# Latent squares summed by TensorE, key tiles taken when the token products leave PSUM, and the second memory tile of the cross values two steps behind the first

## The chip, the cores and the metric

The kernel runs on one core of a Trainium2 chip. The metric is device time in microseconds (us) of one execution, and less is better. The core has a matmul engine (TensorE, PE in the rows; PEld is its weight load), a vector engine (VectorE, DVE), an engine for activations and copies (ScalarE, ACT), a general engine (GpSimd, POOL) and one that issues the transfers (SyncE, SP). Each runs its own program in order and waits on the others through semaphores.

## The reference

```python
for l in range(DEPTH):                                  # DEPTH = 2, SEQ = 512, D_MODEL = 1024
    h = h + hybrid_mixer(rmsnorm(h, attn_norm[l]), ...)
    h = h + memory_cross_attention(rmsnorm(h, cross_norm[l]), rmsnorm(mem, mem_norm[l]), ...)
    h = h + squared_relu_mlp(rmsnorm(h, mlp_norm[l]), mlp_w1[l], mlp_w2[l])
return rmsnorm(h, final_norm)
...
# hybrid_mixer: three groups of heads read one projection n @ w_in
c_q, c_kv, k_r, dq, dk, dv, mq, mk, mv = jnp.split(proj, cuts, axis=-1)
qh = to_heads(rmsnorm(c_q, q_norm) @ w_uq, 96)          # MLA, 6 heads; c_q is 256 wide
kvh = to_heads(rmsnorm(c_kv, kv_norm) @ w_ukv, 128)     # c_kv is 128 wide
k_rope = apply_rope(k_r[:, None], pos)                  # one rotary key for all 6 heads
...
lam = jnp.exp(jnp.sum(lq1 * lk1)) - jnp.exp(jnp.sum(lq2 * lk2)) + lam_init
p = probs(q1, k1) - lam * probs(q2, k2)                 # differential heads, 6
...
# memory_cross_attention: 4 heads over a memory of 256 rows
kv = mem_n @ wkv
```

The third group has 4 block-sparse heads (MoBA). All self-attention is causal, and all arithmetic is float32.

## The kernel before

A float32 product is made of three passes over rounded pieces: every operand is split into an upper half (a cast) and a lower half (the rest, made by a subtraction), and `mm3` issues upper by upper, upper by lower and lower by upper into one PSUM bank. So each weight tile that arrives by DMA is cast by ScalarE (L157), gets its lower half from GpSimd or VectorE (L162), and only then feeds TensorE; there are 5 such pairs of tiles (`w`), 4 buffers for what arrives (`raw`), and 21 pairs for activations (`B`, split at L140/L142, or L144/L145 with a scale). PSUM has three rotating groups of banks: `mm` (3), `s` (3) and `t` (2).

Each layer begins with the mixer. Its projections are generators ("fill") in the order `kv cq tok m0 d0 m1 d1 o0 m2 d2 o1 mem cross`, and the attention units of a group of heads run between their steps once they can. Work that hangs on a product and would stall the engines is put off by a count of "ticks" with `after(ticks, call)`; TensorE's steps count the ticks. Last, a scheduler moves instructions within each engine's program, so the order written is not always the order run.

The stages that the change touches, in the order in which they run:

- `kv` and `cq` make the latents: one tile of 128 rows for kv, two for q. ScalarE copies each product out of PSUM (L760) and squares it (L762). For q, VectorE adds the two squares (L764). Then `column_sums` multiplies the squares by a matrix of ones on TensorE (8 passes with 2 columns), which gives the sum for each token; a reciprocal root follows, and `rows` scales the latent and splits it (kind "lat", lower half on GpSimd).
- `tok` makes, token by token, the differential values and the rotary key: 4 token tiles by 8 steps of the inner dimension by 3 passes of 288 columns, in four PSUM banks (two of `mm`, two of `s`). Its `evict` splits the values out of PSUM (L144, L145), `rotate` turns the key by its position (L825 to L828), and `turn` transposes it (L280 on TensorE), copies it out (L837), splits it (kind "kr") and takes four pairs of `B` for the key tiles.
- `m0`, `m1`, `m2` make q and k of the MLA heads, two heads at a time (L880 scales q by a table and splits it, kind "mq"). Then come the scores of a unit of 128 queries (L638 on VectorE adds the bias and finds the largest, L640 on ScalarE is the exponential with its sum), a reciprocal (L699), a scaling (L700; on GpSimd for the second of the four units), transposes of the probabilities by TensorE (L280), and the product with the values.
- `d0` to `d2` are the differential heads: two score maps per unit, the factor between them from two reciprocals (L1000, L1001), a third one for the end (L1002), and L703, which joins the maps. The factor needs `neg_lam`, which `setup_lambda` makes once from a small transfer: four products of 32 columns (L481), four reductions (L482), an Exp (L483) and four ops with one column.
- `cross` (`cross_memory_steps`, which runs as fill of the mixer) makes keys and values of the memory. For the values, each of two column halves `c` takes two `mm` banks, one for each memory tile `t`, and at each of 8 steps `k` both tiles use one weight tile.

## Time and profile before

| what | value |
|---|---|
| median of 3 runs | 1529.4 us (1529.02 to 1532.49) |
| the profiled execution | 1527.16 us |
| its span, first to last instruction | 1525.3 us |
| TensorE busy | 1481.2 us, 97% of the span |
| VectorE, ScalarE, GpSimd busy | 70%, 56%, 24% |
| mean granted TensorE clock | 0.994 of full speed |

The busy share says which engine has the least room, not what a single stall costs; for that each stage's own rows are needed, and of them the time in which TensorE stood idle and what it waited for. The granted clock is the share of full speed that TensorE was given in a stretch. The profiled execution is 2.2 us under the median.

### The profile page before, as it was taken

The numbers are of one execution on the slowest core, as the hardware profiler recorded it, in microseconds if no ns is written. First come the engines' busy times: TensorE is split into PE (matmuls) and PEld (weight loads), VectorE is DVE, ScalarE is ACT, GpSimd is POOL, SyncE is SP. The second block draws the span as 40 slices with busy tenths as digits, with TensorE's granted clock in tenths as the row PEclk, the third lists the DMA queues.
The fourth block names the chain that finished last, engine by engine and source line by source line (L and its number), as shares of the span: only waits on it lengthen the run. The fifth ranks groups of instructions, "written<-read, shape, count | busy, mean of one in ns | idle before, by whom it ended". The sixth has DMA issues, their size and how long they took to land.

```text
span 1525.3 us, 24601 instructions
## 1 busy us (share of the span) xinstructions
PE 1481.2 (97%) x8648; PEld 1295.4 (85%) x8648; DVE 1060.3 (70%) x2422; ACT 856.9 (56%) x1887; POOL 365.3 (24%) x302
## 2 busy tenths in 40 slices
PE   7899999999999999999999999999999999999997
PEld 6778897888899899998897888878888989899887
DVE  7688888536699666675537898873378976677753
ACT  5666777535566544454446677764366654445441
POOL 2645375442000000000145446644400000000001
PEclk9999999999999999999999999999999999999998
DMA  4434543231223323322224535423212332333331
GB/s 153 127 106 138 153 132 111 77 96 49 87 74 125 111 88 105 100 96 98 96 77 112 150 113 154 118 86 95 98 34 76 106 123 90 104 96 106 111 97 55
DMA packets 90139, 157.24 MB, mean 103 GB/s; under 512 B 12065, under 2 KB 17057, under 8 KB 90017
## 3 DMA queue, kind: packets, MB, share of 16 engines
q1 hardware_dynamic: 89728, 155.63, 33.2%
q8 instruction: 68, 1.11, 0.3%
q14 instruction: 55, 0.44, 0.1%
q10 hardware_dynamic: 288, 0.05, 0.0%
HBM read 136.24 MB, written 2.10 MB: 91 GB/s over the span
## 4 chain that ended last, share of the span: by engine, by line
PE 71%; DVE 10%; issue 9%; ACT 4%; DMA 3%; POOL 2%; SPq 0%; POOLq 0%; DVEq 0%; ACTq 0%
PE mm L277 58%; PE s L277 10%; PE t L280 2%; DMA raw<-w 2%; DVE tmp L638 1%; ACT tmp L640 1%; DVE tmp L703 1%; POOL w L162 1%; DVE pt L663 1%; ACT B L140 1%; DMA raw<-w_in 1%; DVE small L1001 1%; POOL B L142 1%; PE t L277 1%; DVE tmp L261 1%
## 5 line engine op out<-in xcount | busy, mean ns | idle before, releaser
L277 PE MATMUL mm<-B,w 128*128 128x512 f32 (+1 forms) x2490 | 574.4, 386 | 1.3 <-POOL B L142 1.3
L277 PEld LDWEIGHTS mm<-B,w 128*128 128x128 f32 x2490 | 453.0, 189 | 95.1 <-POOL B L142 2.6
L277 PE MATMUL mm<-A,w 128*128 128x512 f32 (+1 forms) x1920 | 386.7, 351 | 6.2 <-ACT A L144 5.8
L157 ACT CAST w<-raw 128x512 fp32r<-128x512 f32 (+1 forms) x372 | 225.1, 607 | 269.6 <-PE mm L277 208.0
L277 PEld LDWEIGHTS mm<-A,w 128*128 128x128 f32 x1920 | 311.8, 190 | 50.7 <-ACT A L144 5.8
L162 POOL TENSOR_TENSOR w<-raw,w 128x512 fp32r<-128x512 f32 (+2 forms) x180 | 228.0, 1273 | 220.1 <-ACT w L157 177.9
L410 POOL TENSOR_TENSOR tmp<-tmp,tmp 128x512 f32<-128x512 f32 (+1 forms) x25 | 30.8, 1234 | 655.7 <-ACT tmp L407 653.6
L162 DVE TENSOR_TENSOR w<-raw,w 128x512 fp32r<-128x512 f32 x192 | 134.4, 700 | 35.5 <-ACT w L157 35.2
L640 ACT ACTIVATE tmp<-tmp,small 128x384 f32<-128x384 f32 (+3 forms) x176 | 99.0, 562 | 66.0 <-DVE small L638 63.2
L1080 DVE TENSOR_TENSOR h<-mm,h 128x512 f32<-128x512 f32 x92 | 63.3, 688 | 70.9 <-PE mm L277 70.6
L140 ACT CAST B<-tmp 128x512 fp32r<-128x512 f32 (+2 forms) x156 | 91.9, 591 | 24.1 <-DVE tmp L680 4.8
L277 PE MATMUL mm<-pt,B 128*128 128x256 f32 x768 | 102.9, 283 | 2.4 <-ACT tmp L1319 2.4
L277 PEld LDWEIGHTS mm<-pt,B 128*128 128x128 f32 x768 | 95.8, 189 | 3.4 <-ACT tmp L1319 3.4
L261 DVE TENSOR_TENSOR tmp<-raw,raw 128x512 f32<-128x512 f32 x64 | 44.0, 688 | 65.9 <-DMA raw<-w 65.9
L264 ACT CAST B<-tmp 128x512 fp32r<-128x512 f32 x96 | 59.5, 620 | 50.8 <-DVE tmp L261 50.8
L142 DVE TENSOR_TENSOR B<-tmp,B 128x512 fp32r<-128x512 f32 (+1 forms) x110 | 75.5, 686 | 12.3 <-ACT B L140 8.3
L280 PE MATMUL t<-ident,tmp 128*128 128x128 f32 (+1 forms) x444 | 74.5, 274 | 9.3 <-DVE tmp L828 3.3
L280 PEld LDWEIGHTS t<-ident,tmp 128*128 128x128 f32 (+1 forms) x444 | 54.2, 140 | 24.8 <-issue 4.2
L142 POOL TENSOR_TENSOR B<-tmp,B 128x512 fp32r<-128x512 f32 (+1 forms) x46 | 61.4, 1340 | 49.7 <-ACT B L140 47.4
L663 DVE TENSOR_TENSOR pt<-t,pt 128x256 fp32r<-128x256 f32 (+1 forms) x192 | 67.1, 370 | 6.3 <-ACT pt L660 5.4
L277 PE MATMUL s<-pt,B 128*128 128x512 f32 (+3 forms) x352 | 71.0, 345 | 0.0
L339 POOL TENSOR_TENSOR small<-small,mhalf 128x4 f32<-128x4 f32 (+2 forms) x19 | 23.4, 1229 | 198.2 <-DVE small L373 174.5
(195 smaller groups left out, 2135.8 us busy)
## 6 DMA issues: line engine op xcount, KB each, us to landing
raw<-w SPq DMA_DIRECT2D x256, 256.0 KB, 2.9
raw<-w_in SPq DMA_DIRECT2D x64, 256.0 KB, 3.0
st<-B SPq DMA_DIRECT2D x144, 64.0 KB, 2.0
raw<-w_ck SPq DMA_DIRECT2D x32, 256.0 KB, 2.9
raw<-w_cv SPq DMA_DIRECT2D x32, 256.0 KB, 2.7
raw<-w_out SPq DMA_DIRECT2D x32, 256.0 KB, 2.7
raw<-w_cq SPq DMA_DIRECT2D x32, 256.0 KB, 2.7
raw<-w_co SPq DMA_DIRECT2D x32, 256.0 KB, 2.6
```

Source lines behind the costliest of these rows:

```text
L140: nc.scalar.copy(hi, x)
L142: eng.tensor_tensor(lo, x, hi.bitcast(F32), ALU.subtract)
L157: self.nc.scalar.copy(w[:, 0, :], raw)
L162: eng.tensor_tensor(w[:, 1, :], raw, w[:, 0, :].bitcast(F32), ALU.subtract)
L261: nc.vector.tensor_tensor(got[name], x, y, op)
L264: nc.scalar.copy(w[:, 0, :], raw)
L277: self.in_order(self.nc.tensor.matmul(out, lhs, rhs, start=start, stop=stop, skip_group_check=open), hold)
L280: self.in_order(self.nc.tensor.transpose(out, x, self.ident))
L410: eng.tensor_tensor(s[:, :n], s[:, :n], self.sq[:, :n], ALU.add)
L640: nc.scalar.activation(t[:, :n], t[:, :n], AF.Exp, bias=st[:, 0:1], scale=-1.0, accum_out=st[:, 1:2])
L663: nc.vector.tensor_tensor(lo, src, hi.bitcast(F32), ALU.subtract)
L1080: nc.vector.tensor_tensor(self.h[m], ps, self.h[m], ALU.add)
```

## The change

`column_sums` takes a list of squares and lets TensorE add them up in PSUM: for q, 16 passes instead of 8, and no add on VectorE. `token_steps` takes three banks of `s` and one of `mm`, and its four pairs of `B` for the keys as soon as `evict` runs; the scores of an MLA head wait (by running ticks) until `turn` has been issued, which is put off by 6 ticks instead of 2. The exponential writes its sum straight into the tile that collects the sums, so one reciprocal over 8 columns serves a pair of differential heads in place of eight over one column, and the scaling of the second unit (L700) goes from GpSimd to VectorE. `setup_lambda` makes its products in one op over 128 columns and one reduction, and is issued at tick 44 in place of 58; the parts of `setup_distances` start at tick 28 in place of 24. In the cross values the second memory tile runs two steps behind the first.

```diff
-    def column_sums(self, sq, ones, ntok, w):
+    def column_sums(self, sqs, ones, ntok, w):
...
         for j in range(ntok):
-            self.mm(o[:, j * w:(j + 1) * w], sq[:, j * P:(j + 1) * P], ones, True, True)
+            for i, sq in enumerate(sqs):
+                self.mm(o[:, j * w:(j + 1) * w], sq[:, j * P:(j + 1) * P], ones, i == 0, i == len(sqs) - 1)
...
-        prod, dots, ex = self.small(64), self.small(4), self.small(4)
-        for l in range(L):
-            for j in range(2):
-                o = (l * 4 + 2 * j) * 32
-                nc.vector.tensor_tensor(prod[:, :32], v[:, o:o + 32], v[:, o + 32:o + 64], ALU.mult)
-                nc.vector.tensor_reduce(dots[:, 2 * l + j:2 * l + j + 1], prod[:, :32], mybir.AxisListType.X, ALU.add)
+        prod, dots, ex = self.small(128), self.small(4), self.small(4)
...
+        nc.vector.tensor_tensor(prod, pairs[:, :, 0, :], pairs[:, :, 1, :], ALU.mult)
+        nc.vector.tensor_reduce(dots, prod, mybir.AxisListType.X, ALU.add)
         nc.scalar.activation(ex, dots, AF.Exp)
...
-        nc.scalar.activation(t[:, :n], t[:, :n], AF.Exp, bias=st[:, 0:1], scale=-1.0, accum_out=st[:, 1:2])
-        return t, st[:, 1:2]
+        nc.scalar.activation(t[:, :n], t[:, :n], AF.Exp, bias=st[:, 0:1], scale=-1.0, accum_out=sums)
+        return t
...
-                (nc.gpsimd if i == 1 else nc.vector).tensor_scalar_mul(t[:, :n], t[:, :n], r)
+                nc.vector.tensor_scalar_mul(t[:, :n], t[:, :n], r)
...
-                if sq is not None:
-                    nc.vector.tensor_tensor(s, s, sq, ALU.add)
-                sq = s
+                sqs.append(s)
...
-            ps = [self.psum("mm"), self.psum("mm"), self.psum("s"), self.psum("s")]
+            ps = [self.psum(t) for t in ("s", "s", "s", "mm")]
...
             def evict():
+                self.keys += [self.pair("B") for _ in range(4)]
...
-                first = self.pair("B")
+                first = self.keys[0]
                 self.split(first[64:128, 0, :], first[64:128, 1, :], u[64:128, :], kind="kr")
-                self.keys.append(first)
-                for j in range(3):
-                    kt = self.pair("B")
+                for kt in self.keys[1:]:
                     nc.sync.dma_start(kt[64:128].bitcast(F32), first[64:128].bitcast(F32))
-                    self.keys.append(kt)
+                self.turned = True
...
                 def terms(e=e):
+                    while not self.turned:
+                        self.tick()
...
-                    nc.vector.reciprocal(r1()[:, 2 * i + e:2 * i + e + 1], s1)
...
-                ot, r = o(), r1()
+                ot, r = o(), self.small(8)
+                nc.vector.reciprocal(r, sums())
...
-            for k in range(KT):
-                w = self.weights(a["w_cv"][l, c * KT + k])
-                for t in range(2):
-                    ts = slice(t * P, (t + 1) * P)
-                    self.mm3(ps[t], (mem[k][0][:, ts], mem[k][1][:, ts]), (w[:, 0, :], w[:, 1, :]),
-                             k == 0, k == KT - 1)
-                    yield 640
+            ws = []
+            for j in range(KT + 2):
+                if j < KT:
+                    ws.append(self.weights(a["w_cv"][l, c * KT + j]))
+                for t, k in ((0, j), (1, j - 2)):
+                    if 0 <= k < KT:
+                        ts, w = slice(t * P, (t + 1) * P), ws[k]
+                        self.mm3(ps[t], (mem[k][0][:, ts], mem[k][1][:, ts]), (w[:, 0, :], w[:, 1, :]),
+                                 k == 0, k == KT - 1)
+                        yield 640
...
-        self.chain_n, self.chain_l, self.chain_d, self.chain_k = 6, 12, 4, 2
+        self.chain_n, self.chain_l, self.chain_d, self.chain_k = 6, 12, 4, 6
...
-            self.after(24 + 2 * n, part)
-        self.after(58, self.setup_lambda)
+            self.after(28 + 2 * n, part)
+        self.after(44, self.setup_lambda)
```

The first place is TensorE's program in layer 0 around the sum of the q latent's squares. `t_89` (now `t_79`) is the sum, `tmp_78` was the sum of both squares; `tmp_51` and `tmp_70` are now the two squares. The products of 288 columns are the token products. Before:

```order
L277 MATMUL mm_79_407<-w_84_413,A_7_129 128x288 x3
L277 MATMUL mm_80_408<-w_84_413,A_7_129 128x288 x3
L277 MATMUL s_81_409<-w_84_413,A_7_129 128x288 x3
L277 MATMUL s_82_410<-w_84_413,A_7_129 128x288 x3
L277 MATMUL mm_79_407<-w_88_438,A_8_132 128x288 x3
L277 MATMUL t_89_447<-ones2_93,tmp_78_404 128x2 x4
L277 MATMUL mm_80_408<-w_88_438,A_8_132 128x288 x3
```

And of the change:

```order
L277 MATMUL s_71_388<-w_54_314,A_5_123 128x288 x3
L277 MATMUL s_72_389<-w_54_314,A_5_123 128x288 x3
L277 MATMUL s_73_390<-w_54_314,A_5_123 128x288 x3
L277 MATMUL mm_74_391<-w_54_314,A_5_123 128x288 x3
L277 MATMUL s_71_388<-w_61_345,A_6_126 128x288 x3
L277 MATMUL s_72_389<-w_61_345,A_6_126 128x288 x3
L277 MATMUL t_79_420<-ones2_93,tmp_51_309 128x2
L277 MATMUL t_79_420<-ones2_93,tmp_70_386 128x2
...
L277 MATMUL s_73_390<-w_61_345,A_6_126 128x288 x3
```

The sums stood behind 13 of the 32 groups of token products and now stand behind 6; the first group that needs an `mm` bank is the fourth, where it was the first.

The second place is GpSimd's program in layer 0, where the lower halves of q and of the rotary key are made. `B_112`, `B_116` and `B_117` are the latents of kv and q, `B_134` (before) and `B_122` (now) the key with its rotary half, `B_140`/`B_143` and `B_142`/`B_145` the two heads of q. Before:

```order
L142 TENSOR_TENSOR B_112_572<-tmp_25_208,B_112_572 128x512
L162 TENSOR_TENSOR w_129_671<-raw_128_669,w_129_671 128x512
L142 TENSOR_TENSOR B_116_604<-tmp_50_307,B_116_604 128x512
L142 TENSOR_TENSOR B_117_608<-tmp_77_402,B_117_608 128x512
L162 TENSOR_TENSOR w_151_752<-raw_150_750,w_151_752 128x512
L162 TENSOR_TENSOR w_159_785<-raw_158_783,w_159_785 128x512
L142 TENSOR_TENSOR B_134_697<-tmp_133_695,B_134_697 64x512
L162 TENSOR_TENSOR w_170_821<-raw_169_819,w_170_821 128x512
L162 TENSOR_TENSOR w_189_900<-raw_188_898,w_189_900 128x256
L142 TENSOR_TENSOR B_140_715<-tmp_139_713,B_140_715 128x512
```

And of the change, from the same place:

```order
L142 TENSOR_TENSOR B_112_575<-tmp_25_208,B_112_575 128x512
L162 TENSOR_TENSOR w_133_678<-raw_132_676,w_133_678 128x512
L142 TENSOR_TENSOR B_116_607<-tmp_50_307,B_116_607 128x512
L142 TENSOR_TENSOR B_117_611<-tmp_69_384,B_117_611 128x512
L162 TENSOR_TENSOR w_156_768<-raw_155_766,w_156_768 128x512
L162 TENSOR_TENSOR w_165_802<-raw_164_800,w_165_802 128x512
L142 TENSOR_TENSOR B_142_718<-tmp_141_716,B_142_718 128x512
L142 TENSOR_TENSOR B_145_730<-tmp_144_728,B_145_730 128x512
L142 TENSOR_TENSOR B_122_636<-tmp_147_738,B_122_636 64x512
```

The rotary key's lower half stood ahead of both halves of q and now stands behind them. On ScalarE, the table load for the exponential and `setup_lambda`'s Exp now stand between the casts of the two heads of q; before they stood behind them.

The third place is TensorE's program in layer 0 where the cross values go from the first column half to the second. `mm_724` and `mm_725` (now `mm_776` and `mm_777`) are the two memory tiles of the first half, `mm_788` and `mm_789` (now `mm_845` and `mm_846`) those of the second, which takes the third bank and then the one of the first tile. Before:

```order
L277 MATMUL mm_724_3070<-w_765_3214,A_593_2486 128x512 x3
L277 MATMUL mm_725_3071<-w_765_3214,A_593_2486 128x512 x3
L277 MATMUL mm_788_3302<-w_775_3250,A_587_2465 128x512 x3
L280 MATMUL t_793_3313<-ident_88,tmp_756_3186 128x128
L277 MATMUL s_794_3317<-st_470_1995,st_444_1896 128x512
L277 MATMUL s_797_3323<-st_470_1995,st_444_1896 128x512
L277 MATMUL mm_788_3302<-w_785_3287,A_587_2465 128x512 x3
L277 MATMUL mm_788_3302<-w_791_3306,A_589_2472 128x512 x3
L277 MATMUL mm_788_3302<-w_802_3339,A_589_2472 128x512 x3
L277 MATMUL mm_789_3303<-w_775_3250,A_587_2465 128x512 x3
```

And of the change:

```order
L277 MATMUL mm_776_3102<-w_820_3240,A_634_2509 128x512 x3
L277 MATMUL mm_777_3103<-w_794_3159,A_632_2502 128x512 x3
...
L277 MATMUL mm_777_3103<-w_806_3192,A_634_2509 128x512 x3
L277 MATMUL mm_777_3103<-w_820_3240,A_634_2509 128x512 x3
L277 MATMUL mm_845_3334<-w_822_3251,A_628_2488 128x512 x3
L280 MATMUL t_850_3345<-ident_88,tmp_813_3224 128x128
L277 MATMUL s_852_3350<-st_499_2009,st_471_1910 128x512
L277 MATMUL s_855_3356<-st_499_2009,st_471_1910 128x512
L277 MATMUL mm_845_3334<-w_833_3287,A_628_2488 128x512 x3
L277 MATMUL mm_845_3334<-w_848_3338,A_630_2495 128x512
L277 MATMUL mm_846_3335<-w_822_3251,A_628_2488 128x512
```

The first tile of the first half now ends nine passes of TensorE (with transposes and scores between them) ahead of the second one, and the last bank is first written after seven passes of the second half instead of twelve.

## Rows read from the trace of the kernel before

**Rows 1.** The page, busy times, shares of the span and instructions.

```profile
PE 1481.2 (97%) x8648; PEld 1295.4 (85%) x8648; DVE 1060.3 (70%) x2422; ACT 856.9 (56%) x1887; POOL 365.3 (24%) x302
```

**Rows 2.** TensorE's waits by cause: total us, times, longest us.

```profile
PE s L277 <- DVE small L638: 4.1, 6, 1.2
...
PE mm L277 <- DVE B L145: 2.2, 2, 1.1
```

**Rows 3.** TensorE from 28 to 56 us: start, length, instructions, idle time and releaser.

```profile
29.43 0.67 PE L277 MATMUL mm<-w,A 128*128 128x288 f32 x3 [0.67 <-ACT tmp L760]
...
37.29 1.02 PE L277 MATMUL t<-ones,tmp 128*128 128x2 f32 x8 [2.86 <-DVE tmp L764]
...
48.62 1.45 PE L277 MATMUL t<-w,B 128*128 128x128 f32 x12
...
51.06 0.97 PE L277 MATMUL mm<-B,w 128*128 128x512 f32 x3 [0.71 <-POOL B L142]
52.32 2.11 PE L277 MATMUL mm<-B,w 128*128 128x512 f32 x8 [0.29 <-POOL B L142]
55.32 0.63 PE L280 MATMUL t<-ident,tmp 128*64 128x128 f32 x4 [0.90 <-DVE tmp L828]
```

**Rows 4.** ScalarE's squares and VectorE's add of the q latent, layer 0.

```profile
31.30 0.58 ACT L760 COPY tmp<-mm 128x512 f32<-128x512 f32 x1
...
32.88 0.63 ACT L762 ACTIVATE tmp<-tmp 128x512 f32<-128x512 f32 x1
...
36.47 0.68 DVE L764 TENSOR_TENSOR tmp<-tmp,tmp 128x512 f32<-128x512 f32 x1
```

**Rows 5.** GpSimd in layer 0, lower halves of the latents.

```profile
41.15 1.27 POOL L162 TENSOR_TENSOR w<-raw,w 128x512 fp32r<-128x512 f32 x1 [0.68 <-ACT w L157]
43.32 0.81 POOL L593 TENSOR_SCALAR_AFFINE_SELECT dneg<-dneg 128x128 f32<-128x128 f32 x1 [0.90 <-DVE small L776]
...
49.74 2.53 POOL L142 TENSOR_TENSOR B<-tmp,B 128x512 fp32r<-128x512 f32 x2
```

**Rows 6.** Three stretches: engines' busy time, granted clock (PEclk), DMA share, GB/s.

```profile
38.00:44.00 6.00, 6.00 (x36) 6.00 (x37) 4.47 (x12) 2.48 (x5) 4.07 (x5) 0.72 0.23 57
76.00:82.00 6.00, 5.60 (x21) 4.73 (x22) 5.03 (x16) 2.58 (x9) 1.01 (x1) 0.72 0.34 80
806.00:812.00 6.00, 5.13 (x18) 4.14 (x19) 3.36 (x6) 2.97 (x5) 3.03 (x3) 0.72 0.30 87
```

**Rows 7.** TensorE in the first MLA heads' units, layer 0.

```profile
68.50 0.44 PE L280 MATMUL t<-ident,tmp 128*128 128x128 f32 x2 [1.18 <-POOL tmp L700]
...
76.40 0.63 PE L280 MATMUL t<-ident,tmp 128*128 128x128 f32 x4 [2.38 <-DVE tmp L700]
```

**Rows 8.** VectorE's wait for the lambda transfer, and ScalarE's table load, layer 0.

```profile
71.27 0.19 DVE L481 TENSOR_TENSOR small<-tmp 128x32 f32<-128x32 f32 x1 [1.39 <-DMA tmp<-lam]
...
61.45 1.28 ACT L640 ACT_TABLE_LOAD   x1
62.75 0.40 ACT L640 ACTIVATE tmp<-tmp,small 128x128 f32<-128x128 f32 x1
```

**Rows 9.** Layer 1: TensorE at the turn of the rotary key; VectorE's rotation.

```profile
806.87 0.63 PE L280 MATMUL t<-ident,tmp 128*64 128x128 f32 x4 [2.43 <-DVE tmp L828]
...
805.31 1.24 DVE L827 TENSOR_TENSOR tmp<-tmp,tmp 128x64 f32<-128x64 f32 x1
```

**Rows 10.** Cross values in layer 0: TensorE's wait, VectorE's lower halves.

```profile
246.09 1.65 PE L277 MATMUL mm<-w,A 128*128 128x512 f32 x6 [1.11 <-DVE B L145]
...
245.30 1.40 DVE L145 SCALAR_TENSOR_TENSOR B<-mm,rcol,B 128x512 fp32r<-128x512 f32 x2
```

**Rows 11.** Lines L1002 and L700: ns shortest/median/longest, first and last start, forms.

```profile
L1002 DVE RECIPROCAL r<-small x48: 135/157/165, 89.5 to 992.3; 128x1 f32<-128x1 f32 x48
...
L700 DVE TENSOR_SCALAR tmp<-tmp,small x60: 276/486/1528, 64.1 to 1015.8; 128x128 f32<-128x128 f32 x20, 128x384 f32<-128x384 f32 x20, 128x512 f32<-128x512 f32 x20
L700 POOL TENSOR_SCALAR tmp<-tmp,small x20: 922/931/1362, 67.5 to 1010.5; 128x256 f32<-128x256 f32 x20
```

More of the change, by code (lines that the diff above doesn't have):

```diff
@@ L627, in stacks, with scores @@
         return tiles, calls
-    def scores(self, i, terms, bias, slope):
+    def scores(self, i, terms, bias, slope, sums):
         nc = self.nc
@@ L694, in start @@
             n = (i + 1) * P
-            got = [self.scores(i, terms(), bias(i), slope) for terms in maps]
-            t, sm = got[0]
             if len(maps) == 1:
-                r = self.small(1)
+                sm, r = self.small(1), self.small(1)
+                t = self.scores(i, maps[0](), bias(i), slope, sm)
                 nc.vector.reciprocal(r, sm)
-                (nc.gpsimd if i == 1 else nc.vector).tensor_scalar_mul(t[:, :n], t[:, :n], r)
+                nc.vector.tensor_scalar_mul(t[:, :n], t[:, :n], r)
             else:
-                t2, s2 = got[1]
-                nc.vector.scalar_tensor_tensor(t[:, :n], t2[:, :n], mixed(i, sm, s2), t[:, :n], ALU.mult, ALU.add)
+                s1, s2 = mixed.sums(i), self.small(1)
+                t, t2 = (self.scores(i, terms(), bias(i), slope, s) for terms, s in zip(maps, (s1, s2)))
+                nc.vector.scalar_tensor_tensor(t[:, :n], t2[:, :n], mixed(s1, s2), t[:, :n], ALU.mult, ALU.add)
             st[i] = t
@@ L752, in latent_steps @@
         def latent_steps(srcs, gain, width):
-            cs = []
-            sq = None
+            cs, sqs = [], []
             for j, src in enumerate(srcs):
@@ L990, in terms, with sums, factor @@
                 return [(q, k[e]) for k in got["k"]]
-            def r1():
-                if "r1" not in oo:
-                    oo["r1"] = self.sb.tile([P, 2 * NQ], F32, tag="r1", name=self.name("r1"), bufs=2)
-                return oo["r1"]
+            def sums():
+                if "sums" not in oo:
+                    oo["sums"] = self.sb.tile([P, 2 * NQ], F32, tag="r1", name=self.name("r1"), bufs=2)
+                return oo["sums"]
             def mixed(e):
-                def factor(i, s1, s2):
+                def factor(s1, s2):
                     r = self.small(2)
@@ L1012, in columns @@
                 def columns():
-                    ms = self.column_sums(sq, self.halves, NQ, 2)
+                    ms = self.column_sums([sq], self.halves, NQ, 2)
                     vv, f = self.small(8), self.small(8)
@@ L1046, in mixer @@
         got = {n: {"moves": []} for n in "d0 d1 d2 m0 m1 m2 o0 o1".split()}
-        self.keys = []
+        self.keys, self.turned = [], False
         steps = {"kv": kv_steps, "cq": cq_steps, "tok": token_steps}
```

14 lines of the change are left out of this document (8 added, 6 removed).

## The prediction

> **What bounds the kernel now.** I read the page first: TensorE is busy 1481.2 of the span's 1525.3 us [rows 1], so a change that leaves its passes alone can gain no more than the 44 us in which it stands idle. Next I read its waits by cause, which say where these 44 us lie. Two groups of rows belong to the parts that change: waits of the scores for VectorE's L638, 4.1 us in six, and of the cross values for L145, 2.2 in two [rows 2]. The others are single waits at the start of a layer, and for these I read TensorE's timeline, where the reader sees a stall and what released it. In layer 0 it waits 0.67 for a copy out of the bank that the token products want, then 2.86 for the sum of the two squares, and before the q products, between them and before the turn of the rotary key 0.71, 0.29 and 0.90 [rows 3]. The square that it waits for is not late by itself: ScalarE has it at 33.51, and VectorE, which is at the distances, adds the two at 36.47 [rows 4]. GpSimd is the next in line: it casts nothing but makes lower halves one after the other, and those of the q latent end at 52.27 [rows 5].
>
> Last I read the granted clock around the three longest waits. Right behind each of them the clock fell: over six microseconds it is 0.72 of full speed, with a stretch at the lower level of 1.2 GHz in place of 2.4 [rows 6]. So a wait of 2.4 to 2.9 us costs another 6 x (1 - 0.72) = 1.7 us, while those of about 1 us show no such loss.
>
> **The change part by part.** The sum is made against the profiled execution, 1527.16 us, which is 2.2 us under the median of 1529.4; I put the same difference on the median.
>
> *Squares, banks and order of the token stage, layer 0.* Removed: the 0.67 (three of the four groups now go to `s` banks, and the `mm` bank is wanted by the fourth), the 2.86, and the clock's 1.7. Added: eight passes, at most 1.02 for eight [rows 3], taken as 1.0. A new wait takes the old one's place: the sum now stands behind 6 groups of token products in place of 13, and needs ScalarE's second square. On ScalarE four weight casts that stood among the copies move ahead of them, so the second square ends after a copy, a row copy and a square of about 0.6 each [rows 4] from 29.9, at about 31.6; TensorE is there at about 30.4: 1.2 us. That leaves 0.67 + 2.86 + 1.7 - 1.0 - 1.2 = 3.0 us, and TensorE comes to the transposing product at 45.6 instead of 48.62 [rows 3]. But GpSimd sets the q products there. From its half at 41.15 to the end of the latents' lower halves at 52.27 (49.74 + 2.53) it takes 11.1 us; the change has the select of 0.81 ahead of this stretch, and with it the 0.90 for which it waited [rows 5]. So the stretch is 9.4 long and ends at about 50.6 if it starts no earlier. Six passes of q remain then, 0.26 each by the eight that took 2.11 [rows 3]: q ends at 52.2 instead of 54.43. **Gain 2.2**, between 0.5 (a new idle time there of about 2 us lowers the clock, 1.7) and 3.0 (GpSimd keeps up).
>
> *The turn.* It is put off by six ticks, not two, and has more cover: 0.90 becomes about 0.3. **Gain 0.6**, between 0 and 0.9. The rotary key's lower half now stands behind those of q on GpSimd. From the first q's scaling at 51.7, ScalarE casts it (0.6), loads the table (1.28), does lambda's Exp (0.2, taken like a VectorE op on one column) and the second cast, the copy and the key's cast (0.6 each), and GpSimd its half (1.27): 56.9. TensorE has 22 passes of other products between the turn and the first scores, 5.3 us, so it wants the key at about 57.8. So this costs nothing, with 0.9 to spare, if the table load takes what it took before: ScalarE's next op began 1.30 after it [rows 8].
>
> On that load the Trainium skill (ScalarE: Activation LUTs, "What ACT_TABLE_LOAD costs") gives about 1283 ns and a drain of 1380, 2.66 us in all. By it the key would come 0.5 late and the sum would be smaller by that; the row shows the load's length but no drain.
>
> *The first heads.* The wait of 1.18 is for the scaling that GpSimd does behind a weight half; on VectorE it takes about 0.4, between the medians of its neighbours. The wait of 2.38 [rows 7] ends with a VectorE op that stands behind lambda's ops, and lambda's first op stood idle 1.39 for its transfer [rows 8]; all of that is now done before the units start. With it goes the clock's 1.7 [rows 6]. Together 5.3; I take **4.2**, since some of the work that waited there will wait elsewhere for a few tenths, and 2.4 as the lower end, where the clock falls anyway. The transfer now has to arrive earlier, and is queued on SP among weight loads; if it is late, VectorE stands with both q behind it.
>
> *Layer 1.* Here the distances do not delay the add, so no stall goes and the eight passes cost 1.0. The turn's wait of 2.43 [rows 9] gets three passes of k as cover, and the keys' lower half moves behind q as above. The 2.43 itself comes from a slow op, 1.24 us for 64 columns, of which the change moves only the neighbours. **Loss 0.4**, between a gain of 1.2 (the clock stays up) and a loss of 2.5.
>
> *Cross values.* In each layer TensorE waits 1.11 (layer 0) or the like for the first tile's lower half, which VectorE makes together with the second's [rows 2, 10]. Now the first tile ends nine passes earlier, its lower half is issued before the second one's, and the bank is written seven passes into the next half. Between its end and that write stand 16 passes, some 4 us at 1.65 for six [rows 10], and VectorE needs 0.7 for one lower half. **Gain 1.8** of 2.2, between 0.5 and 2.2.
>
> *Differential and other heads.* Of the small ops 48 reciprocals of 0.157 go from VectorE, 7.5 us, and six come; 20 scalings of 256 columns come, between 0.28 and 0.49 each, 8 us. In busy time this is nothing; the gain is that reciprocals no longer stand between L638 and the next unit, and the loss is in the MLA and MoBA units. **Gain 1.1** of the 4.1 [rows 2], between -0.5 and 4. The moved scalings took GpSimd 0.93 each; VectorE's own ones took up to 1.528 where the median is 0.486 [rows 11], so some of them stand still beside GpSimd.
>
> The Trainium skill (SBUF — State Buffer, "Who interferes with whom") says why: VectorE in its two-port mode and GpSimd lock each other out for a whole instruction. By it a scaling that meets a GpSimd half (24% of the time) waits about 0.65, 20 x 0.24 x 0.65 = 3 us in all, and a sum with all of that on TensorE's path would be 6.5 and not 9.5; the long ones in the row agree with the rule.
>
> The sum: 2.2 + 0.6 + 4.2 - 0.4 + 1.8 + 1.1 = 9.5 us, so 1517.7 for an execution like the profiled one and 1519.9 for the median.
>
> **The rivals.** *GpSimd and the clock take the start back.* TensorE arrives 3.0 earlier where GpSimd is 1.7 earlier, and stands there some 2 us; the waits behind which the clock fell were 2.38 or longer, those that left it alone 1.18 or shorter [rows 3, 6, 7], so either can be. If it falls, 1.7 is lost, and with the key late and half of the first heads' 4.2 gone, 9.5 - 1.7 - 0.7 - 2.1 = 5.0 remains: about 1524.4. *The change doesn't do what it says:* the 2.38 is ScalarE's queue and not lambda, and stays with its clock: 5.3 remains, 1524.1. *Slower: the cross values run out of weight tiles.* With the second tile two steps behind, a weight tile is held for three steps, and with two ahead all five are taken; one can be cast (0.6) and halved (1.27, [rows 5]) only after its predecessor's last product, 1.9 us and its place in two queues. A step has two groups of three passes, 1.5 us by the 1.65 for six [rows 10], and attention work beside it. For this TensorE shows no wait for weights there now, and the cover is about two steps; against it, 32 steps pay. At 0.24 us in each the other gains, 7.7, are gone; at 0.5 it is 1529.4 - 7.7 + 16 = 1537.7.
>
> **How the numbers follow.** A measurement of this kernel can tell 0.3%, 4.6 us, from no change. My forecast has a chance of 0.66, the start's rival 0.17, the unchanged 2.38 0.07, the weight tiles 0.10. The first is faster; the second lies about the bound, half of it faster (0.08) and half the same (0.09); the third is faster with 0.04 and the same with 0.03; the fourth splits evenly into the same and slower. So faster 0.78, same 0.17, slower 0.05. The bounds taken all together would reach from 1513 (upper ends, 16.6 us) to 1529 (lower ends, about none); they will not all fall on one side, and the range that leaves out 2 in 10 is 1514 to 1527.
>
> **What would show it.** Right: no wait for the add behind the token products, the clock near 1 from 38 to 44 us, TensorE's q products in layer 0 about 2 us earlier and paced by GpSimd, no wait of 2.4 in the first heads, none for L145 in the cross values. Wrong: a clock under 0.8 at the q products; the first scores waiting for GpSimd's L142; VectorE idle for the lambda transfer ahead of q; waits of the cross values for weight halves; L638's waits as before.

## The result and the profile after

The change made the kernel slower: 1537.0 us against 1529.1, a ratio of 1.0051 with a 95% interval of 1.0035 to 1.0068. The forecast was 1519.9. The profiled execution's span is 1534.1 us. Between the two profiled spans lie 8.8 us (1534.1 less 1525.3): 3.4 of idle time on TensorE (47.5 less 44.1) and 5.4 of busy time. Sixteen more passes are some 2 us of the busy time, at the 1.02 for eight of [rows 3]; the rest is not split up further, but at several places below the same passes ran at a lower clock. The page's first row and TensorE's waits by cause (total us, times, longest), which answer to [rows 1, 2]:

```profile
PE 1486.6 (97%) x8664; PEld 1297.1 (85%) x8664; DVE 1067.0 (70%) x2391; ACT 857.5 (56%) x1887; POOL 343.8 (22%) x282
```

```profile
PE s L277 <- DVE tmp L680: 4.3, 8, 1.6
PE s L277 <- DVE small L638: 4.2, 9, 1.3
PE mm L277 <- ACT w L157: 3.1, 4, 1.3
...
PE mm L277 <- POOL w L162: 2.3, 4, 0.6
PE s L277 <- POOL B L142: 2.2, 2, 1.6
...
PE t L277 <- POOL B L142: 1.6, 1, 1.6
...
PE mm L277 <- DVE B L145: 1.0, 1, 1.0
```

Before, this list has no wait for weight tiles, and for L680 it has:

```profile
PE s L277 <- DVE tmp L680: 3.4, 7, 0.7
```

So the two waits for weight tiles (L157, L162), 5.4 us, are new, and those for L638 and L680 did not shrink. TensorE's timeline shows where (start, length, instructions, idle time and releaser):

```profile
31.02 1.72 PE L277 MATMUL t<-ones,tmp 128*128 128x2 f32 x14 [0.74 <-ACT tmp L762]
...
45.06 0.44 PE L277 MATMUL t<-w,B 128*128 128x128 f32 x2 [0.63 <-ACT B L140]
47.06 1.33 PE L277 MATMUL t<-w,B 128*128 128x128 f32 x10 [1.57 <-POOL B L142]
...
49.52 4.16 PE L277 MATMUL mm<-B,w 128*128 128x512 f32 x11 [0.84 <-POOL B L142]
53.84 0.60 PE L280 MATMUL t<-ident,tmp 128*64 128x128 f32 x4 [0.16 <-DVE tmp L827]
...
60.50 1.07 PE L277 MATMUL s<-B,B 128*128 128x128 f32 x6 [0.61 <-POOL B L142]
...
71.40 0.62 PE L280 MATMUL t<-ident,tmp 128*128 128x128 f32 x4
...
86.22 0.73 PE L277 MATMUL mm<-A,w 128*128 128x512 f32 x2 [0.32 <-ACT w L157]
...
101.42 0.44 PE L277 MATMUL s<-st,st 96*128 96x384 f32 x1 [1.28 <-DVE small L638]
...
118.93 1.19 PE L277 MATMUL mm<-A,w 128*128 128x512 f32 x4 [0.49 <-POOL w L162]
...
125.29 1.44 PE L277 MATMUL mm<-w,B 128*128 128x128 f32 x11 [0.53 <-POOL w L162]
```

The start went as forecast: the wait of 2.86 for the add is 0.74 for the square, TensorE comes to the transposing product at 44.4 (45.06 less 0.63) instead of 48.62, stands there for ScalarE's cast and then for GpSimd, and the wait of 2.38 in the first heads [rows 7] is gone (71.40 has none). Then new waits come, for VectorE and for weight tiles. The table follows this through the run. Its rows are starts of the product of a head's probabilities with its values (`s<-pt`, eight passes), which stands in every kernel at the same place of the work; a number is how much later than before a kernel's profiled execution reached it. The second column of numbers is the change with one number put back; the next four are parts of its start (all of it, less the key tiles, and this with six ticks in both layers or one); the rest are single edits, told below.

| reached in before at (us) | the change | turn at 2 ticks | start alone | squares, banks, lambda | with turn at 6 | 6 in layer 1 alone | two steps alone | one step alone | scaling alone | squares, banks, lambda, one step |
|---|---|---|---|---|---|---|---|---|---|---|
| 84.75 | -6.6 | -5.5 | -7.2 | -4.9 | -6.5 | -5.3 | 1.0 | 0.5 | 1.9 | -5.3 |
| 124.13 | -4.0 | -5.8 | -4.6 | -4.7 | -4.0 | -5.1 | 1.0 | 0.5 | 1.7 | -5.1 |
| 139.90 | 0.0 | -3.6 | -2.6 | -4.5 | -1.9 | -5.0 | 1.0 | 0.5 | 5.3 | -5.1 |
| 231.14 | 1.0 | -3.5 | -3.3 | -4.3 | -2.7 | -5.0 | 0.7 | 1.1 | 3.7 | -5.4 |
| 273.21 | 2.5 | -2.5 | -3.1 | -4.0 | -2.5 | -4.8 | 1.1 | -1.2 | 3.9 | -7.7 |
| 832.28 | 4.2 | -2.3 | -1.8 | -4.3 | -1.0 | -3.7 | 1.3 | -2.4 | 2.4 | -7.9 |
| 857.52 | 5.7 | 0.2 | 0.4 | -3.1 | 1.2 | -1.5 | 1.3 | -1.1 | 4.9 | -7.9 |
| 938.00 | 7.9 | 1.2 | 1.5 | -0.3 | 2.3 | 0.0 | 1.1 | -0.8 | 5.6 | -6.7 |
| 975.75 | 7.7 | 1.0 | 3.1 | 0.7 | 2.3 | 0.1 | 0.9 | -1.0 | 5.6 | -7.0 |
| 1018.14 | 8.7 | 2.2 | 3.1 | 0.7 | 2.3 | 0.0 | 2.2 | -3.7 | 5.1 | -9.6 |
| median, less before's | 7.9 | -0.8 | 0.5 | -3.9 | 1.2 | -1.2 | 0.9 | -6.0 | 3.0 | -9.5 |

One execution is not the median: "two steps alone" has the same program as before up to the cross values and yet is 1.0 off at 84.75, and most columns end 1 to 4.5 us above their median, as before's own profiled execution was 2 us under its median. So a column is read by its steps of 2 us and more, and sizes are taken from the medians.

The forecast's 7.0 us for the start of layer 0 was 6.6. It is lost again by 139.90; from 231.14 to the end of the table, with the cross values (231 to 273) and the second layer, the change loses another 7.7 (from 1.0 to 8.7).

### The profile page after: what moved, and what is told of

The parts are those of the page before. It is cut to its first block, busy times and chain, and to the rows that moved or that the text cites. A ratio compares the mean times of both kernels' runs of the same rounds, so it can differ in the third digit from the quotient of the medians.

```text
span 1534.1 us, 24557 instructions
## 1 busy us (share of the span) xinstructions
PE 1486.6 (97%) x8664; PEld 1297.1 (85%) x8664; DVE 1067.0 (70%) x2391; ACT 857.5 (56%) x1887; POOL 343.8 (22%) x282
## 3 DMA queue, kind: packets, MB, share of 16 engines
q8 instruction: 68, 1.11, 0.3%
## 4 chain that ended last, share of the span: by engine, by line
PE 70%; DVE 8%; issue 7%; POOL 6%; ACT 5%; DMA 3%; SPq 1%; POOLq 0%; DVEq 0%; ACTq 0%
PE mm L277 57%; PE s L277 10%; POOL w L162 5%; PE t L280 2%; DMA raw<-w 2%; ACT tmp L640 1%; DVE tmp L638 1%; PE t L277 1%; DVE tmp L261 1%; ACT B L140 1%; DVE pt L663 1%; DVE B L142 1%; ACT w L157 1%; SPq L625 1%; ACT w L264 0%
## 5 line engine op out<-in xcount | busy, mean ns | idle before, releaser
L157 ACT CAST w<-raw 128x512 fp32r<-128x512 f32 (+1 forms) x372 | 224.5, 606 | 265.6 <-PE mm L277 206.8
L162 POOL TENSOR_TENSOR w<-raw,w 128x512 fp32r<-128x512 f32 (+2 forms) x180 | 226.0, 1262 | 236.0 <-ACT w L157 192.2
L162 DVE TENSOR_TENSOR w<-raw,w 128x512 fp32r<-128x512 f32 x192 | 134.3, 699 | 35.4 <-ACT w L157 35.2
L140 ACT CAST B<-tmp 128x512 fp32r<-128x512 f32 (+1 forms) x156 | 92.2, 591 | 29.1 <-DVE tmp L877 6.7
L663 DVE TENSOR_TENSOR pt<-t,pt 128x256 fp32r<-128x256 f32 (+1 forms) x192 | 66.9, 371 | 6.8 <-ACT pt L660 5.2
```

Of the source, the lines that this page charges most:

```text
L140: nc.scalar.copy(hi, x)
L157: self.nc.scalar.copy(w[:, 0, :], raw)
L162: eng.tensor_tensor(w[:, 1, :], raw, w[:, 0, :].bitcast(F32), ALU.subtract)
L663: nc.vector.tensor_tensor(lo, src, hi.bitcast(F32), ALU.subtract)
```

## The experiments

Each kernel was timed in five rounds beside the kernel before, on one chip for each group.

**Parts alone.** The start alone is the change's diff without the hunks of the heads (`scores`, `head_units`, `mixed`, `done_diff`) and of the cross values:

```diff
+    def column_sums(self, sqs, ones, ntok, w):
...
+            ps = [self.psum(t) for t in ("s", "s", "s", "mm")]
...
+                self.keys += [self.pair("B") for _ in range(4)]
...
+        self.chain_n, self.chain_l, self.chain_d, self.chain_k = 6, 12, 4, 6
...
+        self.after(44, self.setup_lambda)
```

> The kernel before with the change's start alone: latent squares summed by TensorE, token banks, key tiles and the later turn, lambda and distances moved. The cross values and the heads' reciprocals and scalings stay as before. Theory A (SyncE's queue gives the start back): in this kernel the loads of weights stand behind and between the moves of stacked tiles, as in the change, so the 6.6 us gained by 84 us are gone again by 140 us with waits for weight halves between 86 and 126 us and a fall of the clock; the median comes out within 2 us of before (1527 to 1531). Theory B (the heads' part loses them): the gain of 6.6 us stays, no waits for weights, median 1522 to 1524.

1529.5 against 1529.0, ratio 1.0006 (0.9996 to 1.0016). The gain at 84 us is there (-7.2) and 4.6 of it are gone by 140, before the second layer takes the rest. The waits for weight halves are there too (0.42, 0.49 and 0.53 between 113 and 126 us), but no fall of the clock behind them: it is 1.00 from 124 to 134. So theory A holds but for the clock, and the gain was not all gone by 140.

The next kernel is this one without the key tiles and the wait for the turn, and with `chain_k` back at 2 (the diff is against the start alone):

```diff
-                self.keys += [self.pair("B") for _ in range(4)]
...
-                    while not self.turned:
-                        self.tick()
...
-        self.chain_n, self.chain_l, self.chain_d, self.chain_k = 6, 12, 4, 6
+        self.chain_n, self.chain_l, self.chain_d, self.chain_k = 6, 12, 4, 2
```

> The kernel before with the squares on TensorE, the four token banks and lambda and distances moved, but key tiles and turn as before (put off by 2 ticks, tiles taken at the turn). SyncE's program then issues five weight loads ahead of the 24 moves of the first differential heads, where the change has two. Theory A: the start's gain is kept past 140 us, median 4 to 7 us below before (1522 to 1525). Theory B: the same as the kernel with the whole start, within 1 us. Both have the eight extra passes of layer 1, 1.0 us.

1525.1, ratio 0.9962 (0.9949 to 0.9976): theory A at its upper end, and the gain stays through all of layer 0. So squares, banks and lambda are worth 3.9 us, and what belongs to the turn and the key tiles costs 4.4.

```diff
+            for j in range(KT + 2):
...
+                for t, k in ((0, j), (1, j - 2)):
```

> The kernel before with the second memory tile two steps behind, nothing else. Theory A (the stagger itself loses: at the change of column halves TensorE waits for a weight tile whose cast stands behind the copy of the second tile, and the clock falls): 2 to 3 us lost in each layer, median 4 to 6 us above before (1533 to 1535), with waits for L157 and L162 at about 246 and 991 us and none for L145. Theory B (that wait comes from where the other parts put the attention units): the 1.1 for L145 is gone in each layer and no wait takes its place, median 1.5 to 2 us below before.

1530.0, ratio 0.9998 (0.9989 to 1.0007). The new waits are there, as theory A has it, and the old one is gone; but the time is neither theory's. Together they come to about nothing, and in the profiled execution the clock fell behind them in one layer only (below).

```diff
-        nc.scalar.activation(t[:, :n], t[:, :n], AF.Exp, bias=st[:, 0:1], scale=-1.0, accum_out=st[:, 1:2])
+        nc.scalar.activation(t[:, :n], t[:, :n], AF.Exp, bias=st[:, 0:1], scale=-1.0, accum_out=sums)
...
-                (nc.gpsimd if i == 1 else nc.vector).tensor_scalar_mul(t[:, :n], t[:, :n], r)
+                nc.vector.tensor_scalar_mul(t[:, :n], t[:, :n], r)
...
-                    nc.vector.reciprocal(r1()[:, 2 * i + e:2 * i + e + 1], s1)
```

> The kernel before with the heads' part alone: sums written straight, one reciprocal over eight columns for a pair of differential heads, the second unit's scaling on VectorE. Theory A: it loses little, 0 to 2 us, by waits of the scores and transposes for VectorE (L638, L680, L959) in place of those for GpSimd. Theory B (this part makes the loss between 820 and 950 us in layer 1, 3.7 us, and the like in layer 0): 5 to 8 us above before (1534 to 1537). By my prediction: 1.1 us below before.

1531.1, ratio 1.0015 (1.0005 to 1.0025): a loss of 2.0, the upper end of theory A, and the other side of my 1.1 of gain.

**The change less one part.** First the stagger at one step, alone:

```diff
-            for j in range(KT + 2):
+            for j in range(KT + 1):
...
-                for t, k in ((0, j), (1, j - 2)):
+                for t, k in ((0, j), (1, j - 1)):
```

> The kernel before with the second memory tile one step behind the first, not two, and nothing else. Theory A (with two steps all five weight tiles are held, so the tile wanted right after the change of column halves is cast only behind the copy of the second memory tile): with one step that cast stands ahead of the copy, the wait of 1.28 and 0.62 us for L157 and L162 is gone, and so is the 1.1 for L145; median 1.5 to 3 us below before (1526 to 1527.5). Theory B (any stagger costs, by where the attention units fall): no better than two steps, within 1 us of before.

1522.9 against 1528.9, ratio 0.9961 (0.9946 to 0.9977): theory A, and twice what it gave. Then the change without the stagger (its `range(KT + 2)` loop as before), without the heads' hunks, and without the key tiles and the turn:

> The whole change without the stagger of the cross values. If the parts add up, the start (+0.5) and the heads (+2.0) give 1531.5. Theory A (parts meet: behind the stagger the clock falls in both layers in the whole change, and heads and start together starve more): 1532 to 1533.5, so the stagger costs 4 to 5 us in the whole change where alone it cost about nothing. Theory B (the heads cost more after the changed start): above 1534.5, with the stagger worth under 2.

1534.5, ratio 1.0036 (1.0023 to 1.0049): between the theories. The stagger of two steps costs the whole change 2.3 to 2.6 (the first when each kernel is set against the before timed beside it), and the parts do not add up: start and heads alone gave 2.5, together 5.6.

> The whole change without the heads' part. If the parts add up, the start (+0.5) and the stagger (-0.3 to +1) give 1529.5 to 1530. Theory A: 1532 to 1533, as the stagger costs more behind the changed start. Theory B (the heads' part costs 6 to 8 us behind the changed start): 1529 to 1530.5.

1531.2, ratio 1.0021 (1.0012 to 1.0029): between the theories; the heads' part costs 5.6 to 5.8 there.

> The whole change, but key tiles taken at the turn as before, the turn put off by 2 ticks and no wait for it; the loads of weights keep their place ahead of the moves on SyncE's queue. If the parts add up: -3.9 (squares, banks, lambda), +2.0, about 0: 1527. Theory A (the order on SyncE's queue costs 4 to 6 us): 1530 to 1533, well under the 1537 of the change. Theory B (the queue's order does not matter in the whole change): 1535 or more.

1528.5, ratio 0.9998 (0.9989 to 1.0008): beyond theory A. Of the change's 7.9, this part makes 8.

**One number.** In this kernel the change keeps its key tiles and its wait for the turn:

```diff
-        self.chain_n, self.chain_l, self.chain_d, self.chain_k = 6, 12, 4, 6
+        self.chain_n, self.chain_l, self.chain_d, self.chain_k = 6, 12, 4, 2
```

> The whole change with one number put back: the turn of the rotary key is put off by 2 ticks and not 6. SyncE's program then has five weight loads ahead of the first 24 moves again. Theory A (that number costs the 8 us, by SyncE's order in layer 0 and the late key): as the change without its key tiles, 1527 to 1530. Theory B (the key tiles taken early and the wait for the turn cost them): 1535 or more.

1527.8 against 1528.6, ratio 0.9993 (0.9983 to 1.0003): theory A. The reverse, 6 in the kernel with squares, banks and lambda:

> Squares, banks and lambda (1525.1 by itself, 3.9 below before) with that one number at 6 and nothing else of the change. SyncE's program has two loads ahead of 21 moves, as the change has. Theory A: the 3.9 are gone, 1528 to 1532, with waits for weight halves between 86 and 126 us. Theory B: within 1 us of 1525.

1529.8, ratio 1.0005 (0.9996 to 1.0013): theory A again, 4.7 lost. The two best parts together:

> Squares, banks and lambda as in the change, the turn at 2 ticks, and the second memory tile one step behind. If the two add up (3.9 and 5.9): 1519 to 1520, faster than both kernels. If the gain of the one step was in part chance of where the clock fell: 1521 to 1523.

1519.1, ratio 0.9930 (0.9918 to 0.9943): they add up. And the heads' part in halves, first without the line of the scaling, then with it alone:

> The kernel before with the sums written straight and one reciprocal over eight columns, the second unit's scaling left on GpSimd. Theory A (the scalings on VectorE, slow beside GpSimd, are the heads' 2 us): within 1 us of before, or 1 to 2 below it. Theory B (the order of the reciprocals is): 1530.5 to 1531.5, as the whole heads' part.

1528.6, ratio 1.0002 (0.9991 to 1.0013): theory A, the reciprocals are free.

```diff
-                (nc.gpsimd if i == 1 else nc.vector).tensor_scalar_mul(t[:, :n], t[:, :n], r)
+                nc.vector.tensor_scalar_mul(t[:, :n], t[:, :n], r)
```

> The kernel before with the second unit's scaling on VectorE and nothing else. The heads' part cost 2.0 and the reciprocals alone nothing (1528.6). Theory A (the scalings are the 2 us, though they take VectorE 0.35 and GpSimd 0.93): 1530.5 to 1531.5. Theory B (only both together lose): within 1 us of before. By my prediction it gains by the wait of 1.18 at 68.5 us.

1531.5 against 1528.5, ratio 1.0017 (1.0006 to 1.0027): theory A, all of it.

**How the six ticks lose.** In layer 1 alone:

```diff
-                self.after(self.chain_k, lambda: turn(t))
+                self.after(6 if l else 2, lambda: turn(t))
```

> Squares, banks and lambda, with the turn at 6 ticks in the second layer alone (2 in the first); SyncE's program in layer 0 is the good one. With 6 in both layers the median was 1529.8, with 2 in both 1525.1. Theory A (about half of the loss lies in layer 1, where the key's lower half stands behind both halves of q): 1527 to 1528, with waits of about 1.0, 1.0 and 1.6 us at the start of layer 1 in place of 2.5. Theory B (all of it is layer 0's queue): 1525.

1527.4, ratio 0.9992 (0.9983 to 1.0001): theory A, 2.3 of the 4.7 lie in layer 1 (2.8 of 5.1 when each kernel is set against the before timed beside it). The other half was tried by SyncE's order, put in and taken out:

First, in `fetch` of the kernel with squares, banks and lambda and the turn at 2, each load is made to stand behind the move issued before it; then, in `qk_steps` of the whole change, the moves of layer 0 are no longer issued a tick apart but only when a later step asks for those that are left:

```diff
+        if self.last_move is not None:
+            self.tc.add_manual_dep(ins.ins, self.last_move, ...)
```

> Squares, banks and lambda with the turn at 2 ticks (3.9 below before), and one order added: in layer 0 a load of weights is issued by SyncE only behind the moves of stacked tiles that were asked for before it, so loads stand between moves there as in the change. Theory A (SyncE's order is how the turn's 6 ticks lose in layer 0): the gain at 84 us is gone by 140 us with waits for weights; 2 to 5 us over 1525, so 1527 to 1530. Theory B (it is the late rotary key by itself): within 1 us of 1525.

```diff
-                    self.after(j, lambda some=some: move(some))
+                    if l:
+                        self.after(j, lambda some=some: move(some))
```

> The whole change, but in layer 0 the moves are issued only when the first scores ask for them; SyncE's program then has seven loads ahead of the first 24 moves, where the change has two. Theory A: no waits for weights between 86 and 126 us, 2 to 5 us below the change (1532 to 1535), unless the moves are late themselves, which would show as waits of the first differential scores for transfers. Theory B: within 1 us of 1537.

1551.7 (ratio 1.0149, 1.0130 to 1.0167) and 1552.0 (1.0157, 1.0138 to 1.0176). Both miss every range. The first order is more mixed than the change's, with waits for weight tiles from 60 to 300 us of 6.3 (L157) and 4.0 us (L162; lines as before). In the second the moves are late as well, not only the order changed: the second group is issued from 139 us, where before issues its second group from 99. Against the kernels that they were made from, the first loses some 27 us and the second 15. So how this queue is filled can cost many us, but neither run shows that the change's own order costs its 2 us or so.

**The change mended**, with these three edits (turn at 2, one step, scaling on GpSimd) and nothing else:

> The whole change with the three places put right that the runs point to: the turn put off by 2 ticks, the second memory tile one step behind, the second unit's scaling left on GpSimd. If these three are the whole loss, it comes out like squares, banks and lambda with the one step (1519.1, 9.5 below before): 1518 to 1521. If the early key tiles or the reciprocals cost something in this company: 1522 to 1526.

1521.4 against 1530.2, ratio 0.9942 (0.9927 to 0.9957): three edits turn 7.9 of loss into 8.8 of gain. The time lies between the two ranges expected; its interval overlaps that of 0.9930 (0.9918 to 0.9943), so whether the early key tiles and the reciprocals cost the last 0.7 us can't be told. In its profile TensorE has no wait for weight tiles and none for L607, which the scaling brought (below).

## Why the prediction was wrong

**Squares, banks, turn and first heads of layer 0: the mechanism and the total right, the split in part luck.** Forecast 2.2, 0.6 and 4.2, together 7.0; at 84.75 the change is 6.6 ahead. GpSimd set the q products as worked out; its rows (start, length, instructions) show the halves of the latents ending at 50.72 where I had 50.6, and the key's behind those of q:

```profile
48.20 2.52 POOL L142 TENSOR_TENSOR B<-tmp,B 128x512 fp32r<-128x512 f32 x2
...
59.18 1.27 POOL L142 TENSOR_TENSOR B<-tmp,B 64x512 fp32r<-64x512 f32 x1 [0.62 <-ACT B L140]
```

The rivals' price was there too: TensorE stood 0.63, 1.57 and 0.84 and the clock fell. These are windows of the change (length, busy time of PE, PEld, DVE, ACT, POOL with counts, granted clock, DMA share, GB/s):

```profile
48.00:54.00 6.00, 5.00 (x18) 3.44 (x18) 5.60 (x18) 3.47 (x12) 3.95 (x4) 0.72 0.41 123
124.00:134.00 10.00, 9.27 (x50) 7.74 (x49) 5.15 (x18) 5.64 (x14) 7.40 (x6) 0.83 0.56 176
244.00:252.00 8.00, 6.09 (x24) 4.44 (x23) 6.42 (x15) 5.61 (x15) 5.36 (x4) 0.79 0.34 116
996.00:1004.00 8.00, 6.35 (x25) 5.03 (x26) 6.14 (x14) 5.05 (x12) 5.37 (x4) 0.79 0.39 103
```

At 48 to 54 us it is 0.72, as behind the long waits [rows 6]. So q ended at 53.68 (49.52 and 4.16), 0.8 earlier than before and not 2.2; the turn's wait went from 0.90 to 0.16, 0.7 gained; and the rest of the 6.6, the first heads, gave 5.1 and not 4.2. The misses cancel, which is why the total is so near.

The key was 0.61 late (60.50 in TensorE's rows) where I had 0.9 to spare. GpSimd stood idle 0.62 for its cast, so the halves of q did not hold it; ScalarE did:

```profile
54.53 0.62 ACT L140 CAST B<-tmp 128x512 fp32r<-128x512 f32 x1
55.17 1.28 ACT L484 ACT_TABLE_LOAD   x1
56.47 0.21 ACT L484 ACTIVATE small<-small 128x4 f32<-128x4 f32 x1
...
57.81 0.58 ACT L140 CAST B<-mm 64x512 fp32r<-64x512 f32 x1
58.42 0.62 ACT L140 CAST B<-tmp 64x512 fp32r<-64x512 f32 x1
```

It cast the first q at 54.53 where I had 51.7, as q itself was late, and one cast that I had not counted (57.81) stood ahead of the key's. The table load took 1.28 and the next op began 1.30 after it, as in [rows 8]. The Trainium skill (ScalarE: Activation LUTs, "What ACT_TABLE_LOAD costs") adds a drain of 1380 ns to it; from the end of the op ahead (55.15) to the next one (56.47) this trace has 1.32 us in all, so it shows no drain, and the key's lateness is no sign of one.

**The six ticks: the step that failed most.** I weighed them as cover for the turn, gain 0.6 in layer 0, and gave layer 1 a loss of 0.4 with 2.5 as the bound. They cost 4.7 us by themselves and 9.2 in the whole change (1537.0 against 1527.8); set against the before timed beside each kernel it is 5.1 and 8.8. What I had wrong is that a later turn only adds cover: in layer 0 the ticks gain 1.6 up to 84.75 (-6.5 against -4.9 in the table, more than the 0.6) and are 2.6 behind by 139.90 (-1.9 against -4.5). In layer 1 they change the waits at the turn and later ones. TensorE in the kernel with 6 ticks in layer 1 alone:

```profile
801.72 0.96 PE L277 MATMUL mm<-B,w 128*128 128x512 f32 x3 [0.99 <-DVE B L145]
803.65 0.62 PE L280 MATMUL t<-ident,tmp 128*64 128x128 f32 x4 [0.97 <-DVE tmp L825]
...
809.37 0.73 PE L277 MATMUL s<-B,B 128*128 128x128 f32 x4 [1.59 <-POOL B L142]
...
843.42 0.33 PE L277 MATMUL s<-st,st 96*128 96x128 f32 x1 [1.15 <-DVE small L638]
...
850.85 0.44 PE L277 MATMUL s<-st,st 96*128 96x384 f32 x1 [0.91 <-DVE small L638]
```

0.99, 0.97 and 1.59 stand where 2.43 stood [rows 9], and where the kernel with two ticks (squares, banks and lambda) has 2.53 and 0.17: 0.9 more. Behind them the wait for L638 at 843 is nothing new, since the kernel with two ticks has 1.50 there; the 0.91 at 851 it does not have. From 273.21 to 857.52 this kernel loses 3.3 by the table and the one with two ticks about 1, which fits the 2.3 to 2.8 of the medians. Later in layer 1 the latter loses more (0.7 at the end), but its profiled execution was the slowest of its five. Why the scores are late at 851 was not followed further.

In layer 0 the ticks change what I did not look at: SyncE's program. Its rows for the change, and then for before (start, length, instructions; `st` are the moves of stacked tiles, `raw` the loads):

```profile
60.48 1.98 SPq L840 DMA_DIRECT2D B<-B  x3
62.56 2.53 SPq L151 DMA_DIRECT2D raw<-w_in  x2
65.87 13.90 SPq L625 DMA_DIRECT2D st<-B  x21
79.81 0.58 SPq L151 DMA_DIRECT2D raw<-w_in  x1
```

```profile
58.67 1.83 SPq L843 DMA_DIRECT2D B<-B  x3
60.61 7.28 SPq L151 DMA_DIRECT2D raw<-w_in  x4
...
69.19 18.24 SPq L625 DMA_DIRECT2D st<-B  x24
```

Before, four loads stood ahead of 24 moves; now two do, the next stands behind 21 moves of 0.66 us each at 79.81, and TensorE waits for a tile's cast at 86.22. The loads of later heads are as late, which gives the waits for L162 at 118.93 and 125.29, and behind them the clock of 0.83 from 124 to 134. Of this queue I had written only that the lambda transfer stands in it among weight loads. That this order is the cause in layer 0 is likely and not shown, since no run changed the order alone (above). For it speaks that the start alone and squares, banks and lambda with six ticks have the same order (two loads, 21 moves, one load) and waits for L162 of 0.4 to 0.5, while the kernels with two ticks in layer 0 (before, squares, banks and lambda, and the change with that number put back) have four or five loads ahead of the 24 moves and no wait for a weight tile from 84 to 140 us. The wait for L638 hardly grew there (1.28 at 101.42, where before has 1.09).

**The scaling on VectorE: sized by the wrong rows.** I took it as 0.28 to 0.49 each and as a gain of 1.18. It costs 3.0 us alone (0.9 to 4.1 by the interval). The kernel with the scaling alone shows it on VectorE, then on GpSimd, then what TensorE waits for and the clock behind it:

```profile
135.74 1.45 DVE L700 TENSOR_SCALAR tmp<-tmp,small 128x256 f32<-128x256 f32 x1
137.11 1.25 DVE L344 TENSOR_TENSOR small<-small,small 128x8 f32<-128x8 f32 x1
...
139.27 0.68 DVE L607 TENSOR_TENSOR B<-t,B 128x512 fp32r<-128x512 f32 x1
```

```profile
135.75 1.28 POOL L142 TENSOR_TENSOR B<-tmp,B 128x512 fp32r<-128x512 f32 x1
```

```profile
140.10 0.30 PE L280 MATMUL t<-ident,tmp 128*128 128x128 f32 x1 [1.96 <-DVE B L607]
```

```profile
140.00:148.00 8.00, 7.90 (x35) 6.66 (x36) 7.72 (x18) 5.54 (x14) 4.02 (x3) 0.79 0.16 52
```

The scaling of 256 columns (0.28 to 0.49 by its neighbours) took 1.45, beside a GpSimd half that ran from 135.75 to 137.03. L607 came late, TensorE waited 1.96 and the clock fell to 0.79. (The op on 8 columns between them took 1.25 beside the next half, but before it took 1.21 at this place, so it is no part of the loss.) Of the 20 scalings 16 took 0.34 to 0.44, as I had them, and four 1.01 to 1.45. Waits of 1.8 to 2.2 for L607 stand in the heads alone, in the change with the turn at 2 ticks and in the change without the key tiles as well, and neither in before nor in the mended change. The wait of 1.18 did shrink, to 0.44, but the one of 2.38 behind it became 3.02. The Trainium skill's rule (SBUF — State Buffer, "Who interferes with whom") agrees with this length of 1.45, and I had its price as 3 us at the worst and did not take it. The reciprocals, from which I had the gain of 1.1, are worth nothing that can be measured (1528.59 against 1528.61).

**The cross values: the cover that I named as a rival, at one place and not at every step.** I forecast 1.8 and gave the weight tiles 0.10, at 0.24 us and more in each of 32 steps. In the change TensorE and then ScalarE:

```profile
243.63 0.86 PE L277 MATMUL mm<-w,A 128*128 128x512 f32 x3
245.78 0.73 PE L277 MATMUL mm<-w,A 128*128 128x512 f32 x2 [1.29 <-ACT w L157]
247.14 2.08 PE L277 MATMUL mm<-w,A 128*128 128x512 f32 x4 [0.62 <-POOL w L162]
```

```profile
244.55 0.67 ACT L144 ACTIVATE B<-mm,rcol 128x512 fp32r<-128x512 f32 x1
245.12 0.60 ACT L157 CAST w<-raw 128x512 fp32r<-128x512 f32 x1
```

The 1.11 for L145 [rows 10] is gone, and 1.29 and 0.62 stand in its place, once in each layer: the tile wanted next is cast (L157) only behind the copy of the second memory tile (L144). The clock of 0.79 from 244 and from 996 adds up to 8 x 0.21 = 1.7 each. That this rival's 1537.7 lies beside the measured 1537.0 is chance: it was worked out from waits in all 32 steps. With one step TensorE has this at the same place:

```profile
244.58 1.66 PE L277 MATMUL mm<-w,A 128*128 128x512 f32 x6 [0.51 <-DVE B L145]
```

0.51 and no fall of the clock, so 0.6 less than the 1.11 of [rows 10]; the waits around it for L680 and L663, 1.3 before (236 to 264 us), are 0.4. That is 1.5 us in layer 0, and the table gives 2.3 and 2.7 for the two stretches of cross values. The median's 6.0 is more than I can find in one profile.

**The sum** failed by parts that meet. Alone the start, the heads and the stagger come to 0.5, 2.0 and 0.9, 3.4 together, and the change has 7.9. One such meeting may be in the clock: in the profiled executions it fell behind the stagger in one layer when alone and in both in the change. Another is that of the six ticks with the rest of the change, 5.1 alone and 8.8 in it. Why they meet stays open. I did not price a meeting at all.

## What to carry to other kernels

A number that puts off one step moves others: when a scheduler lays out the queues, compare the order of every queue, the one that issues the transfers first, before the step itself is priced. A gain at the start of a stage is only kept if what feeds the next stage is not already at its pace; look at which loads stand behind which moves there. Hold one weight tile less than there are buffers at the place where a copy and a cast share an engine, and count an op that moves to an engine by its longest rows at the places where it will meet the neighbour's work (here four of twenty), not by its median alone.

## What the runs showed that I had not expected

The clock fell behind less than I took for needed: behind waits of 1.29 and 0.62 close together in the change, not behind 1.28 and 0.62 at the same place in layer 0 of the kernel with two steps alone (clock 1.00 from 244 to 252), but behind 1.55 and 0.62 in its layer 1 (0.79 from 988 to 996). And it did not always fall behind what I took for enough: at the turn of layer 1, 2.53 left it at 1.00 in squares, banks and lambda (802 to 816), 2.44 left it at 1.00 with one step alone, and behind 2.53 in the mended change it was 0.72 (800 to 806), as behind 2.43 in before [rows 6, 9]. Nor were the forecast's three waits the three longest: before has one of 5.8 at the start of the run. So the price of 1.7 that I put on each long wait is not fixed: the same idle time costs 0 or up to 1.7 us, and a program that is unchanged up to a place can reach it 1 us sooner or later from one execution to the next.
